# A block of ffn, two mixers and ffn on one core: first unit's weights beside the input, written places for the norm's sums, gates' sigmoids among pair 0's products

## The chip, the cores and the metric

One NeuronCore of a Trainium2 chip runs the kernel. The time is that of the device for one execution, in microseconds (us); smaller is better. Each figure of a kernel's time is the median of several executions. The engines carry the names of the profile: PE is TensorE (PEld its loads of the stationary operand), ACT ScalarE, DVE VectorE, POOL GpSimd, and SP SyncE, which here only issues DMAs.

## What is computed

One layer, `x` with 512 frames of 1024 numbers, all in fp32:

```python
x = x + 0.5 * swiglu(rms_norm(x, ffn1_norm), ffn1_w1, ffn1_w3, ffn1_w2)   # silu(h@w1)*(h@w3) @ w2, 2816 hidden
h = rms_norm(x, mix_norm)
p = h @ w_in                      # r, k, v (512 each), codes w, a, g; FoX q, k, v, f; gates (2048)
p_rwkv = token_shift(p[:, :SHIFT_COLS], shift_mu)        # u + (prev - u) * mu
y_a = rwkv7_mixer(p_rwkv, ...) @ rwkv_proj               # 8 heads of 64, delta-rule state
y_b = fox_mixer(p[:, SHIFT_COLS:...], ...) @ fox_proj    # attention with forget gates
x = x + (sigmoid(g_a) * y_a + sigmoid(g_b) * y_b) @ w_out
x = x + 0.5 * swiglu(rms_norm(x, ffn2_norm), ffn2_w1, ffn2_w3, ffn2_w2)
return rms_norm(x, final_norm)
```

In the RWKV mixer the decay is made from `w0 + tanh(w_code) @ w_up`, and `a = sigmoid(a0 + a_code @ a_up)`. The kernel makes the first through a sigmoid too: these two groups, four column blocks each, are its eight "pz" products.

## The kernel before

All activations lie transposed: a column block `c` of x is a tile of 128 features by 512 frames, and there are eight. A product is exact to fp32 by splitting: each operand is a high part in fp32r and the low part that is left, and `mm3` (L124 to L127) issues three matmuls, high by high (L125), high weight by low activation (L126), low weight by high activation (L127). A product of 128 columns of a weight matrix with the eight blocks is thus 24 matmuls of 512 columns (`Norm.cols`, L203). Its weights come by `load_raw` (L104: one DMA on SP's queue into one of 3 buffers "raw") and `split_w` (L113: ACT casts the high part "whi" at L117, DVE subtracts the low part "wlo" at L118; 2 buffers each).

The order of work on each engine is set by a scheduler that simulates the program and issues what is ready; `tc.issue_after(x)` holds an instruction behind x, `keep_in_program_order` holds a row of them in written order.

- **Start (L216 to L372).** Seven warm products on PE (L219). Then the first hidden unit of ffn1 (128 columns of w1 in the PSUM bank f0, of w3 in f1) is made column block by column block while x arrives. Every instruction of this block passes through `Queued` (L228, recorded at L234), which chains the instructions of one engine in the written order. `turn(c)` transposes block c of x on PE (tile xtp, four transposes); `x_copy` copies it to SBUF on ACT (xT); `x_hi` makes the high part xh (even blocks on DVE, odd ones on ACT) and `x_lo` the low part xl on DVE, both scaled by the norm's gain and read from xtp; `w_hi`, `w_lo` split the unit's weights by halves; `mul(i, c)` issues the three matmuls of block c on bank i. `square` and `add` sum the squares for the norm (acc). The first unit's raw and split weights take buffers of the same rings as all others.
- **ffn1 (L430 to L492).** Unit j has pa (w1) and pb (w3). Its scale by the norm (rstd) is applied behind the product, in `hidden`, so the sum of squares over the features is only needed then: `Norm.finish` (L193) splits acc (`exact`, L135: shi on ACT, slo on DVE), sums it by two matmuls with ones (ssum, L139 and L140), and makes rstd by Ln and Exp on ACT. `finish` is called behind pa of unit 1; where its two matmuls stand among the products is the scheduler's choice. `during` loads 18 small parameter rows (L399 to L415) on SP's queue at unit 2. After 22 units come eight products with w2 (pd), whose results go into x and, by `mix_add`, into the next norm's operands.
- **Mix (L537 to L581).** `mix.finish`, the products of the codes (pl, 72 and 96 columns), then the eight pz (L579), each read by a sigmoid on ACT (L580), kept in that order, and behind them the table load for Ln and Exp (L581). PSUM has 8 banks: 2 in the pool pm (pl, pk, pgt, pa, pd), 3 in pr (pb, ssum, one half of the pz), 3 in pf (the other half).
- **Pairs (`step`, L634).** For each of four pairs of heads: `column` (L611) makes the products k, r, v (tile pk), each scaled by rstd into u (L614, DVE) and shifted in time (L532 on ACT, L533 on DVE); a gate product pgt follows. The sigmoids' results are summed along time by DVE (scan, L650, with the mask cmask that POOL sets at L588, L589), exponentials follow on ACT (L655, L656), and keys and queries go to the tiles BK and G, which the products gp (L694) read.

Behind this come the recurrence with the attention, the projections, ffn2 (the same `ffn`, with `finish` behind unit 0) and the last norm.

## Time and profile before

| | |
|---|---|
| median of 3 executions | 1208.77 us (1207.17 to 1209.34) |
| the profiled execution | 1206.81 us, of which the span of the trace is 1205.1 us |
| mean granted clock of PE | 0.997 |
| moved by DMA | 122.54 MB, 102 GB/s |
| ffn1's first unit ends, its pa of unit 1 begins | 23.55 us |
| last pd of ffn1 ends, pl begins | 380.34 us |
| pair 0: first k product / first gate product | 392.27 / 414.42 us |
| recurrence begins | 561.33 us |

A row of a timeline has: start in us, length in us, engine, line of the code, operation, tiles (out<-in), shape, xcount, and in brackets how long the engine was idle just before and what released it. In a group's row the idle time before and its releasers stand behind the bar. A matmul's length in the timeline overlaps with the next one's; the distance of starts is its pace.

### The profile page before, as it was taken

The numbers are of one execution on the slowest core, as the hardware profiler recorded it, in microseconds if no ns is written. First come the engines' busy times: TensorE is split into PE (matmuls) and PEld (weight loads), VectorE is DVE, ScalarE is ACT, GpSimd is POOL, SyncE is SP. The second block draws the span as 40 slices with busy tenths as digits, with TensorE's granted clock in tenths as the row PEclk, the third lists the DMA queues.
The fourth block names the chain that finished last, engine by engine and source line by source line (L and its number), as shares of the span: only waits on it lengthen the run. The fifth ranks groups of instructions, "written<-read, shape, count | busy, mean of one in ns | idle before, by whom it ended". The sixth has DMA issues, their size and how long they took to land.

```text
span 1205.1 us, 15863 instructions
## 1 busy us (share of the span) xinstructions
PE 1183.4 (98%) x6332; PEld 950.3 (79%) x6332; DVE 661.5 (55%) x990; ACT 454.9 (38%) x733; POOL 94.7 (8%) x141
## 2 busy tenths in 40 slices
PE   8999999999999999999999999999999999999997
PEld 6788888888887788887767776778888888888887
DVE  6554445443334788686756655766554545543232
ACT  5322222222223754346876655523222222222221
POOL 2100000001111111311000011111000000000110
PEclk9999999999999999999999999999999999999999
DMA  6333333323333334345112135633323233323331
GB/s 183 90 101 95 97 105 88 103 81 114 114 114 93 94 101 116 114 127 129 40 56 89 54 97 164 192 106 88 105 88 105 88 105 91 102 84 92 96 97 71
DMA packets 210296, 122.54 MB, mean 102 GB/s; under 512 B 9998, under 2 KB 202574, under 8 KB 210222
## 3 DMA queue, kind: packets, MB, share of 16 engines
q1 hardware_dynamic: 204222, 108.67, 31.0%
q0 software_dynamic: 3760, 12.06, 3.1%
q8 instruction: 50, 0.82, 0.3%
q10 hardware_dynamic: 2240, 0.79, 0.3%
q14 instruction: 24, 0.20, 0.1%
HBM read 110.82 MB, written 10.68 MB: 101 GB/s over the span
## 4 chain that ended last, share of the span: by engine, by line
PE 93%; DVE 3%; ACT 1%; issue 1%; DMA 0%; DVEq 0%; ACTq 0%
PE pd L127 7%; PE pd L126 7%; PE pd L125 7%; PE pb L127 6%; PE pb L125 6%; PE pb L126 6%; PE pa L127 6%; PE pa L126 6%; PE pa L125 6%; PE pgt L125 3%; PE pgt L127 2%; PE pgt L126 2%; PE pk L125 2%; PE pk L127 2%; PE pk L126 2%; PE ppj L125 1%
## 5 line engine op out<-in xcount | busy, mean ns | idle before, releaser
L117 ACT CAST whi<-raw 128x1024 fp32r<-128x1024 f32 (+2 forms) x196 | 195.2, 997 | 617.7 <-PE pa L126 176.6
L118 DVE TENSOR_TENSOR wlo<-raw,whi 128x1024 fp32r<-128x1024 f32 (+2 forms) x196 | 227.0, 1158 | 136.9 <-ACT whi L117 136.9
L125 PE MATMUL pb<-xh,whi 128*128 128x512 f32 x344 | 134.0, 390 | 1.2 <-ACT whi L117 1.2
L127 PE MATMUL pa<-xh,wlo 128*128 128x512 f32 x344 | 134.2, 390 | 0.8 <-DVE wlo L234 0.5
L127 PE MATMUL pb<-xh,wlo 128*128 128x512 f32 x344 | 134.0, 389 | 0.5 <-DVE wlo L118 0.5
L125 PE MATMUL pa<-xh,whi 128*128 128x512 f32 x344 | 134.0, 389 | 0.2 <-ACT whi L234 0.2
L126 PE MATMUL pa<-xl,whi 128*128 128x512 f32 x344 | 133.9, 389 | 0.0
L126 PE MATMUL pb<-xl,whi 128*128 128x512 f32 x344 | 133.8, 389 | 0.0
L127 PE MATMUL pd<-hh,wlo 128*128 128x512 f32 x330 | 130.8, 396 | 0.0
L125 PE MATMUL pd<-hh,whi 128*128 128x512 f32 x330 | 130.3, 395 | 0.0
L126 PE MATMUL pd<-hl,whi 128*128 128x512 f32 x330 | 130.3, 395 | 0.0
L439 DVE TENSOR_TENSOR fb<-pb,rstd 128x512 f32<-128x512 f32 x43 | 29.7, 691 | 133.7 <-PE pb L127 133.7
L125 PEld LDWEIGHTS pb<-xh,whi 128*128 128x128 f32 x344 | 64.5, 188 | 15.3 <-ACT whi L117 2.0
L127 PEld LDWEIGHTS pa<-xh,wlo 128*128 128x128 f32 x344 | 64.5, 188 | 15.1 <-DVE wlo L234 1.0
L127 PEld LDWEIGHTS pb<-xh,wlo 128*128 128x128 f32 x344 | 64.6, 188 | 14.4 <-DVE wlo L118 1.0
L125 PEld LDWEIGHTS pa<-xh,whi 128*128 128x128 f32 x344 | 64.6, 188 | 14.0 <-ACT whi L234 0.7
L126 PEld LDWEIGHTS pa<-xl,whi 128*128 128x128 f32 x344 | 64.6, 188 | 13.4
L126 PEld LDWEIGHTS pb<-xl,whi 128*128 128x128 f32 x344 | 64.6, 188 | 13.4
L126 PEld LDWEIGHTS pd<-hl,whi 128*128 128x128 f32 x330 | 62.0, 188 | 14.9
L125 PEld LDWEIGHTS pd<-hh,whi 128*128 128x128 f32 x330 | 62.0, 188 | 14.6
L127 PEld LDWEIGHTS pd<-hh,wlo 128*128 128x128 f32 x330 | 62.0, 188 | 14.6
L435 DVE TENSOR_TENSOR fa<-pa,rstd 128x512 f32<-128x512 f32 x43 | 29.7, 692 | 73.2 <-PE pa L127 73.2
(380 smaller groups left out, 1960.7 us busy)
## 6 DMA issues: line engine op xcount, KB each, us to landing
raw<-in_ffn_w_dram SPq DMA_DIRECT2D x116, 512.0 KB
raw<-in_w_in_dram SPq DMA_DIRECT2D x40, 512.0 KB
raw<-in_ffn_w_dram SPq DMA_DIRECT2D x15, 384.0 KB
raw<-in_w_out_dram SPq DMA_DIRECT2D x8, 512.0 KB
raw<-in_ffn_w_dram SPq DMA_DIRECT2D x9, 256.0 KB
gsave<-gs SPq DMA_DIRECT2D x9, 256.0 KB
xin<-in_x_dram SPq DMA_DIRECT2D x8, 256.0 KB
xsave<-xT POOLq DMA_DIRECT2D x8, 256.0 KB, 2.3
```

Source lines behind the costliest of these rows:

```text
L117: (hi_eng or act).copy(hi[:], raw[:])
L118: (eng or dve).tensor_tensor(lo[:], raw[:], hi[:].bitcast(F32), op=ALU.subtract)
L125: pe.matmul(ps, whi, xhi, start=first, stop=False)
L126: pe.matmul(ps, whi, xlo, start=False, stop=False)
L127: return pe.matmul(ps, wlo, xhi, start=False, stop=last)
L435: dve.tensor_tensor(a[:], pa[:], nrm.rstd[:], op=ALU.mult)
L439: dve.tensor_tensor(b[:], pb[:], nrm.rstd[:], op=ALU.mult)
```

## The change

Three edits.

**First unit.** Its raw and split weights get tiles of their own in the pool x0, so the rings of `load_w` are free: w1 and w3 of unit 1 are loaded right behind the input, and both are split within the queued block. For blocks 2 to 7 ACT copies xtp to SBUF first, and xh and xl are made from the copy. The transposes run one block ahead (`turn(4)` before `mul(0, 2)`), and the squares come later. Five warm products in place of seven. The parameter rows are issued behind the last weight load that stands before them in the program.

**Norm sums.** `finish` is divided: `parts` adds, casts and subtracts; `finish(behind)` issues both ssum matmuls behind a given matmul, and the next product is issued behind them (`[summed]`, the holes of `cols`). The places: ffn1 behind the last but one matmul of pa of unit 1, mix behind pl's 72 columns, ffn2 behind pa of unit 0.

**Pair 0.** Its products k and r are written ahead of the pz, and pz i is issued behind the matmul i of r (`spread`); `step(0)` no longer makes them.

How PE's order stands in the first unit before: xtp are the transposes of a block, f0 and f1 the two banks, xh2 and xl2 the parts of block 2.

```order
L234 MATMUL xtp_212<-ident_78,xin3_136 128x128 x4
L234 MATMUL f0_147<-xh2_202,whi_143 128x512
L234 MATMUL f0_147<-xl2_204,whi_143 128x512
L234 MATMUL f0_147<-xh2_202,wlo_145 128x512
L234 MATMUL f1_148<-xh2_202,whi_144 128x512
L234 MATMUL f1_148<-xl2_204,whi_144 128x512
L234 MATMUL f1_148<-xh2_202,wlo_146 128x512
L234 MATMUL xtp_230<-ident_78,xin4_137 128x128 x4
L234 MATMUL f0_147<-xh3_223,whi_143 128x512
```

And in the changed kernel, from the same place:

```order
L244 MATMUL xtp_210<-ident_78,xin3_134 128x128 x4
L244 MATMUL xtp_215<-ident_78,xin4_135 128x128 x4
L244 MATMUL f0_145<-xh2_201,fwhi0_141 128x512
L244 MATMUL f0_145<-xl2_203,fwhi0_141 128x512
L244 MATMUL f0_145<-xh2_201,fwlo0_143 128x512
L244 MATMUL f1_146<-xh2_201,fwhi1_142 128x512
L244 MATMUL f1_146<-xl2_203,fwhi1_142 128x512
L244 MATMUL f1_146<-xh2_201,fwlo1_144 128x512
L244 MATMUL xtp_231<-ident_78,xin5_136 128x128 x4
L244 MATMUL f0_145<-xh3_227,fwhi0_141 128x512
```

Two blocks are transposed before the products of block 2, and from there on each transpose stands a block further ahead.

On SP's queue three weight loads (w3 of unit 1, w1 and w3 of unit 2) now stand between w1 of unit 1 and the first of the parameter rows; before, the rows followed w1 of unit 1 directly.

PE at the end of pair 0's r product before (pk_2943 is r, pk_2993 is v):

```order
L579 MATMUL pz_2851<-codes_2734,uw_330 128x512
L579 MATMUL pz_2857<-codes_2734,uw_330 128x512
L579 MATMUL pz_2863<-codes_2734,uw_330 128x512
L127 MATMUL pk_2943<-xh7_2709,wlo_2947 128x512
L579 MATMUL pz_2869<-codes_2734,uw_330 128x512
L579 MATMUL pz_2872<-codes_2734,ux_331 128x512
L125 MATMUL pk_2993<-xh0_2052,whi_2996 128x512
L126 MATMUL pk_2993<-xl0_2053,whi_2996 128x512
```

And in the changed kernel (pk_2884 is r, pk_2991 v, pgt_3026 the gate):

```order
L129 MATMUL pk_2884<-xh7_2707,wlo_2888 128x512
L604 MATMUL pz_2919<-codes_2732,uw_338 128x512
L604 MATMUL pz_2922<-codes_2732,ux_339 128x512
L604 MATMUL pz_2925<-codes_2732,uw_338 128x512
L604 MATMUL pz_2928<-codes_2732,ux_339 128x512
L604 MATMUL pz_2931<-codes_2732,uw_338 128x512
L604 MATMUL pz_2934<-codes_2732,ux_339 128x512
L127 MATMUL pk_2991<-xh0_2050,whi_2994 128x512
L128 MATMUL pk_2991<-xl0_2051,whi_2994 128x512
...
L604 MATMUL pz_2937<-codes_2732,uw_338 128x512
L129 MATMUL pk_2991<-xh7_2707,wlo_2995 128x512
L127 MATMUL pgt_3026<-xh0_2050,whi_3029 128x512
L604 MATMUL pz_2940<-codes_2732,ux_339 128x512
L128 MATMUL pgt_3026<-xl0_2051,whi_3029 128x512
```

Six pz follow r's last matmul; the seventh stands ahead of v's last matmul and the eighth behind the gate's first.

ACT at the same place before (whi_2996 is v's weights, whi_3031 the gate's; L580 the sigmoids, L532 the shift's first half):

```order
L117 CAST whi_2996<-raw_2994 128x1024
L117 CAST whi_3031<-raw_3029 128x1024
L580 ACTIVATE G30_2728<-pz_2851,par_116 128x512
L580 ACTIVATE G30_2728<-pz_2854,par_116 128x512
L580 ACTIVATE G31_2729<-pz_2857,par_116 128x512
L580 ACTIVATE G31_2729<-pz_2860,par_116 128x512
L580 ACTIVATE BK3_2733<-pz_2863,par_116 128x512
L580 ACTIVATE BK3_2733<-pz_2866,par_116 128x512
L580 ACTIVATE spare0_2736<-pz_2869,par_116 128x512
L580 ACTIVATE spare0_2736<-pz_2872,par_116 128x512
L581 ACT_TABLE_LOAD
L532 ACTIVATE spare1_2737<-u_2923,omu_2744 128x512
```

And in the changed kernel (whi_3029 is the gate's, whi_3120 those of pair 1's k; L605 the sigmoids):

```order
L119 CAST whi_3029<-raw_3027 128x1024
L550 ACTIVATE spare1_2735<-u_2915,omu_2742 128x512
L605 ACTIVATE G30_2726<-pz_2919,par_116 128x512
L605 ACTIVATE G30_2726<-pz_2922,par_116 128x512
L605 ACTIVATE G31_2727<-pz_2925,par_116 128x512
L605 ACTIVATE G31_2727<-pz_2928,par_116 128x512
L605 ACTIVATE BK3_2731<-pz_2931,par_116 128x512
L605 ACTIVATE BK3_2731<-pz_2934,par_116 128x512
L119 CAST whi_3120<-raw_3118 128x1024
L605 ACTIVATE spare0_2734<-pz_2937,par_116 128x512
L605 ACTIVATE spare0_2734<-pz_2940,par_116 128x512
L606 ACT_TABLE_LOAD
```

The gate's cast and the shift of r stand ahead of the sigmoids, and a cast stands between the sixth and the seventh.

The diff, cut to its core:

```diff
+    loads = []
+
     def load_raw(aps, kt, n):
         raw = wp.tile([P, kt, n], F32, tag="raw", name="raw", bufs=3)
         for c0, src in aps:
-            nc.sync.dma_start(raw[:, :, c0:c0 + src.shape[1]],
-                              src.rearrange("(k p) c -> p k c", p=P))
+            loads.append(nc.sync.dma_start(raw[:, :, c0:c0 + src.shape[1]],
+                                           src.rearrange("(k p) c -> p k c", p=P)))
         return raw
...
-        def finish(s):
+        def parts(s, a=act, v=dve):
+            if s.last is not None:
+                v.tensor_tensor(s.acc[:], s.acc[:], s.last[:], op=ALU.add)
+            s.sum = tmp("shi", dt=F32R), tmp("slo", dt=F32R)
+            a.copy(s.sum[0][:], s.acc[:])
+            v.tensor_tensor(s.sum[1][:], s.acc[:], f32(s.sum[0][:]), op=ALU.subtract)
+
+        def finish(s, behind):
             ps = bank("ssum", pr)
-            if s.last is not None:
-                dve.tensor_tensor(s.acc[:], s.acc[:], s.last[:], op=ALU.add)
-            exact(ps[:], onesr, s.acc[:])
+            with tc.issue_after(behind.ins):
+                for i in range(2):
+                    done = pe.matmul(ps[:], onesr[:], s.sum[i][:], start=i == 0, stop=i == 1)
             ln = tmp("rln")
             ln_act(ln[:], ps[:], bias=epsr[:, 0:1], scale=1.0 / D)
             s.rstd = xp.tile([P, T], F32, tag="rstd", name="rstd")
             act.activation(s.rstd[:], ln[:], AF.Exp, scale=-0.5)
+            return done
...
     warm = bank("warm", pf)
-    for _ in range(7):
+    for _ in range(5):
         pe.matmul(warm[:, 0:P], ones[:], ones[:], start=True, stop=True)
...
         xin = [x0.tile([P, NB, P], F32, name=f"xin{c}") for c in range(KD)]
-        fraw = [wp.tile([P, KD, P], F32, tag="raw", name="raw", bufs=3) for _ in range(2)]
-        fhi, flo = [[wp.tile([P, KD, P], F32R, tag=f"w{n}", name=f"w{n}", bufs=2) for _ in range(2)] for n in ("hi", "lo")]
+        fraw = [x0.tile([P, KD, P], F32, name=f"fraw{i}") for i in range(2)]
+        fhi, flo = [[x0.tile([P, KD, P], F32R, name=f"fw{n}{i}") for i in range(2)] for n in ("hi", "lo")]
         first = [bank(f"f{i}") for i in range(2)]
...
             nrm.hi[c] = xp.tile([P, T], F32R, tag=f"xh{c}", name=f"xh{c}")
+            from_ = (xps if c < 2 else xT)[c][:]
             if c % 2:
-                qact.activation(nrm.hi[c][:], xps[c][:], AF.Copy, scale=pc(PAR_FFN1 + c))
+                qact.activation(nrm.hi[c][:], from_, AF.Copy, scale=pc(PAR_FFN1 + c))
             else:
-                qdve.tensor_scalar(nrm.hi[c][:], xps[c][:], pc(PAR_FFN1 + c), None, op0=ALU.mult)
+                qdve.tensor_scalar(nrm.hi[c][:], from_, pc(PAR_FFN1 + c), None, op0=ALU.mult)
         def x_lo(c):
             nrm.lo[c] = xp.tile([P, T], F32R, tag=f"xl{c}", name=f"xl{c}")
-            qdve.scalar_tensor_tensor(nrm.lo[c][:], xps[c][:], pc(PAR_FFN1 + c), f32(nrm.hi[c][:]),
+            from_ = (xps if c < 2 else xT)[c][:]
+            qdve.scalar_tensor_tensor(nrm.lo[c][:], from_, pc(PAR_FFN1 + c), f32(nrm.hi[c][:]),
                                       op0=ALU.mult, op1=ALU.subtract)
...
         x_copy(1)
+        x_copy(2)
         x_hi(2)
         x_lo(2)
-        x_copy(2)
         square(0)
         square(1)
         add()
         turn(3)
+        turn(4)
         mul(0, 2)
         mul(1, 2)
+        x_copy(3)
         x_hi(3)
         x_lo(3)
-        x_copy(3)
+        turn(5)
+        mul(0, 3)
+        mul(1, 3)
+        x_copy(4)
+        x_hi(4)
+        x_lo(4)
         w_hi(0, 1)
         w_hi(1, 1)
-        turn(4)
-        mul(0, 3)
-        mul(1, 3)
-        x_hi(4)
-        x_lo(4)
-        x_copy(4)
         w_lo(0, 1)
         w_lo(1, 1)
-        square(2)
-        turn(5)
...
-        x_copy(7)
+        add()
+        second = [split_w(load_raw([(0, ffn1_w1[0][:, P:2 * P])], KD, P), KD, P, qdve, hi_eng=qact)]
         mul(0, 7)
         mul(1, 7)
-        for c in range(4, KD):
+        for c in range(3, KD):
             square(c)
             add()
         nrm.last = None
+        nrm.parts(qact, qdve)
+        second.append(split_w(load_raw([(0, ffn1_w3[0][:, P:2 * P])], KD, P), KD, P, qdve, hi_eng=qact))
...
                 for ps, w in ((pa, w1), (pb, w3)):
-                    wh, wl = first[1] if j == 1 and first and ps is pa else load_w([(0, w[0][:, c0:c0 + P])], KD, P)
-                    nrm.cols(ps[:], wh, wl, P)
-                    if ps is pa and j == 1 and first:
-                        nrm.finish()
-                        hidden(0, *first[0])
-                if j == 0:
-                    nrm.finish()
+                    if j == 1 and first:
+                        wh, wl = first[1][ps is pb]
+                    else:
+                        wh, wl = load_w([(0, w[0][:, c0:c0 + P])], KD, P)
+                    mms = nrm.cols(ps[:], wh, wl, P, [summed] if summed else [])
+                    summed = None
+                    if ps is pa and nrm.rstd is None:
+                        if first is None:
+                            nrm.parts()
+                        summed = nrm.finish(mms[-1 if first is None else -2])
+                        if first:
+                            hidden(0, *first[0])
                 if j in during:
-                    with tc.issue_after(pin.ins):
+                    with tc.issue_after(pin.ins), tc.issue_after(loads[-1].ins):
                         during[j]()
...
-    ffn(nrm, ffn1_w1, ffn1_w3, ffn1_w2, mix_add, {2: load_params, 4: masks, 10: place_params}, (first, ahead))
+    ffn(nrm, ffn1_w1, ffn1_w3, ffn1_w2, mix_add, {2: load_params, 4: masks, 10: place_params}, (first, second))
...
-        mix.finish()
+        psa, psg = bank("pl"), bank("pl")
+        mms = mix.cols(psa[0:72, :], *load_w([(0, W[:, COL_W:COL_W + 64]), (64, W[:, COL_F:COL_F + 8])], KD, 72), 72)
+        mix.parts()
+        summed = mix.finish(mms[-1])
         tc.keep_in_program_order(act.preload_act_table_set("sigmoid_and_others"))
-        psa, psg = bank("pl"), bank("pl")
-        mix.cols(psa[0:72, :], *load_w([(0, W[:, COL_W:COL_W + 64]), (64, W[:, COL_F:COL_F + 8])], KD, 72), 72)
-        mix.cols(psg[0:96, :], *load_w(win(COL_G, 96), KD, 96), 96)
+        mix.cols(psg[0:96, :], *load_w(win(COL_G, 96), KD, 96), 96, [summed])
         rc = rp.tile([P, NB], F32, name="rc")
...
         zslots = [h.rearrange("p c a t -> p (c a t)") for h in zslots] + spare[0:2]
+        spread = []
+        for o, c0, mu in ((spare[2], DA, 4), (spare[3], 0, 0)):
+            ps = bank("pk")
+            spread = mix.cols(ps[:], *load_w(win(c0), KD, P), P)
+            shifted(o, normed(ps), P, PAR_MU + mu)
         za = []
         for p in range(NP):
             za.append((zslots[2 * p], zslots[2 * p + 1]))
             for i, (w_, x_, par0, o) in enumerate(((uw, lw, PAR_W0, zslots[2 * p]), (ux, lx, PAR_A0, zslots[2 * p + 1]))):
                 ps = bank("pz", (pr, pf)[i])
-                pe.matmul(ps[:], w_[0:96, p * P:(p + 1) * P], x_[0:96, :], start=True, stop=True)
+                with tc.issue_after(spread[2 * p + i].ins):
+                    pe.matmul(ps[:], w_[0:96, p * P:(p + 1) * P], x_[0:96, :], start=True, stop=True)
                 tc.keep_in_program_order(act.activation(o, ps[:], AF.Sigmoid, bias=pc(par0 + p)))
...
             BK = BKs[p]
-            column(DA, p, k, 4)
+            if p:
+                column(DA, p, k, 4)
             kk = prep("kk", p)
...
-            mms = column(0, p, r, 0)
+            mms = column(0, p, r, 0) if p else spread
             ps = bank("pn", pf)
```

More of the change, by code (lines that the diff above doesn't have):

```diff
@@ L325 @@
         turn(3)
+        turn(4)
         mul(0, 2)
         mul(1, 2)
+        x_copy(3)
         x_hi(3)
         x_lo(3)
-        x_copy(3)
+        turn(5)
[4 more added lines that the diff above has]
+        x_lo(4)
         w_hi(0, 1)
         w_hi(1, 1)
-        turn(4)
-        mul(0, 3)
-        mul(1, 3)
-        x_hi(4)
-        x_lo(4)
-        x_copy(4)
         w_lo(0, 1)
         w_lo(1, 1)
-        square(2)
-        turn(5)
+        turn(6)
         mul(0, 4)
         mul(1, 4)
+        x_copy(5)
         x_hi(5)
         x_lo(5)
-        x_copy(5)
-        add()
-        square(3)
-        turn(6)
+        turn(7)
         mul(0, 5)
         mul(1, 5)
+        x_copy(6)
         x_hi(6)
         x_lo(6)
-        x_copy(6)
-        add()
-        turn(7)
+        square(2)
         mul(0, 6)
         mul(1, 6)
+        x_copy(7)
         x_hi(7)
         x_lo(7)
-        ahead = split_w(load_raw([(0, ffn1_w1[0][:, P:2 * P])], KD, P), KD, P, qdve, hi_eng=qact)
-        x_copy(7)
+        add()
+        second = [split_w(load_raw([(0, ffn1_w1[0][:, P:2 * P])], KD, P), KD, P, qdve, hi_eng=qact)]
         mul(0, 7)
         mul(1, 7)
-        for c in range(4, KD):
+        for c in range(3, KD):
             square(c)
```

1 line of the change is left out of this document (added).

## The prediction

> **What bounds the kernel now.** I read the first part of the page (busy time by engine) and the chain that ended last, then the busy time by stretch, and then the timeline of the stretches in which TensorE isn't full.
>
> ```profile
> span 1205.1 us, 15863 instructions
> PE 1183.4 (98%) x6332; PEld 950.3 (79%) x6332; DVE 661.5 (55%) x990; ACT 454.9 (38%) x733; POOL 94.7 (8%) x141
> PE 93%; DVE 3%; ACT 1%; issue 1%; DMA 0%; DVEq 0%; ACTq 0%
> ```
>
> PE carries 93% of the chain: only PE time taken out of the span counts. The view by stretch, in us: length, then busy time (instructions) of PE, PEld, DVE, ACT, POOL, then the granted clock.
>
> ```profile
> 10.43:23.55 13.12, 12.19 (x58) 8.59 (x56) 8.23 (x14) 8.83 (x16) 0.00 (x0) 1.00 0.67 171
> 23.55:51.03 27.48, 24.85 (x103) 18.68 (x103) 17.13 (x22) 13.94 (x18) 8.48 (x7) 1.00 0.30 85
> 404.45:414.42 9.97, 8.31 (x29) 6.00 (x28) 7.78 (x9) 9.92 (x17) 2.57 (x10) 0.83 0.23 64
> 414.42:500.00 85.58, 85.58 (x535) 69.81 (x534) 73.91 (x102) 46.94 (x63) 19.72 (x30) 1.00 0.35 104
> ```
>
> Busy PE time includes waits inside the pipeline, so I count starts. A gate product (24 matmuls of 512 columns) starts at the first of these rows, the next product at the second:
>
> ```profile
> 414.42 0.39 PE L125 MATMUL pgt<-xh,whi 128*128 128x512 f32 x1
> ...
> 419.86 0.39 PE L125 MATMUL pk<-xh,whi 128*128 128x512 f32 x1
> ```
>
> 5.44/24 = 0.227 us for each, the pitch of a full PE. Four transposes and one matmul lie between the first and third of these rows:
>
> ```profile
> 10.65 0.60 PE L234 MATMUL xtp<-ident,xin 128*128 128x128 f32 x4
> 11.01 0.48 PE L234 MATMUL f<-xh,whi 128*128 128x512 f32 x1
> 11.32 0.40 PE L234 MATMUL f<-xl,whi 128*128 128x512 f32 x1
> ```
>
> 0.67 − 0.227 = 0.44 for four, 0.11 each. The counts of the stretches hold instructions that still run from before the border: one, one and two. So the work and the loss are:
>
> - 10.43 to 23.55: 37 × 0.227 + 20 × 0.11 = 10.6 of 13.12: **2.5 lost**
> - 23.55 to 51.03: 102 × 0.227 = 23.15 of 27.48: **4.3 lost**
> - 404.45 to 414.42: 27 × 0.227 = 6.13 of 9.97: **3.8 lost**
>
> These 10.6 us are all that the change can aim at; in the stretch from 414.42 PE is busy throughout.
>
> **First unit.** What waits there:
>
> ```profile
> 13.73 0.50 PE L234 MATMUL f<-xl,whi 128*128 128x512 f32 x1 [0.32 <-DVE xl L234]
> 21.87 0.50 PE L234 MATMUL f<-xl,whi 128*128 128x512 f32 x1 [0.28 <-DVE xl L234]
> 23.55 0.50 PE L125 MATMUL pa<-xh,whi 128*128 128x512 f32 x1 [0.24 <-ACT whi L234]
> 24.81 0.50 PE L127 MATMUL pa<-xh,wlo 128*128 128x512 f32 x1 [0.53 <-DVE wlo L234]
> 37.36 0.50 PE L125 MATMUL pb<-xh,whi 128*128 128x512 f32 x1 [0.94 <-ACT whi L117]
> 38.62 0.50 PE L127 MATMUL pb<-xh,wlo 128*128 128x512 f32 x1 [0.53 <-DVE wlo L118]
> 13.71 0.59 ACT L234 COPY xT<-xtp 128x512 f32<-128x512 f32 x1 [0.84 <-DVE xl L234]
> ```
>
> The first two wait for the low part of a column of x, the next four for split weights. The last row shows a cost of the old order: the copy stood idle behind DVE's reading of the same PSUM tile. The prices (all in the last number but one: count, total and mean ns, or min/median/max):
>
> ```profile
> L234 ACT COPY xT<-xtp 128x512 f32<-128x512 f32 x8 | 4.6, 588 | 4.1 <-DVE xl L234 4.1
> L234 ACT ACTIVATE xh<-xtp,par 128x512 fp32r<-128x512 f32 x4 | 2.7, 686 | 1.7 <-PE xtp L234 1.7
> L171 DVE TENSOR_SCALAR xh<-xT,par 128x512 fp32r<-128x512 f32 x8 | 3.9, 485 | 0.2
> L172 DVE SCALAR_TENSOR_TENSOR xl<-xT,par,xh x8: 742/1781/1781, 275.0 to 383.2; 128x512 fp32r<-128x512 f32 x8
> L234 DVE TENSOR_TENSOR wlo<-raw,whi 128x512 fp32r<-128x512 f32 x3 | 2.0, 683 | 0.0
> ```
>
> Now a column goes copy, high, low: 0.59 + 0.69 + 0.74 = 2.0 us, one copy longer than from PSUM. But a transpose runs one column ahead: between it and its first product stand two columns' products and one or two transposes, 12 × 0.227 + 0.44 = 3.2 us, where before there was one column's 6 × 0.227 + 0.44 = 1.8. That covers 2.0 with 1.2 left. Throughput holds too: for two columns in 3.6 us, ACT has two copies, one high part and two half casts of 0.62 (the 128x1024 one of 1.05 for a half more), 3.1; DVE two low parts, one high part and two 0.68 subtractions, 3.35. That is tight in DVE, once; I leave 0.4 of the 2.5.
>
> The low part's price hangs on POOL: 742 ns alone, 1781 in most runs of ffn1's end. In 10.43 to 23.55 POOL has no instruction, so I take 0.74; at 1.78 DVE would need 5.4 in 3.6 us, and six columns would cost up to 6 × 0.9 = 5.4 us. The Trainium skill, "SBUF — State Buffer", section "Who interferes with whom", says that a VectorE instruction with two SBUF inputs contends with a GpSimd instruction that reads SBUF. This speaks against reading the copy instead of PSUM; the trace agrees in kind (742 against 1781), and where POOL is empty the rule gives the same 0.74.
>
> The weights of units 1 and 2 then load directly behind the input, ahead of the small parameter rows, which take SP's queue from here to the second line's end:
>
> ```profile
> 10.90 1.72 SPq L399 DMA_DIRECT2D rows<-in_mix_norm_dram  x1
> ...
> 22.25 0.42 SPq L415 DMA_DIRECT2D loraw<-in_rwkv_a_up_dram  x1
> ```
>
> PE: first unit ends at 10.43 + 10.6 + 0.4 = 21.4; pa of unit 1 (5.4) 26.9, where the two ssum matmuls stand; pb must have its low weights at 27.8. ACT after the last column: one cast, five squares, the sum's cast, the second cast: 1.05 + 5 × 0.63 + 0.62 + 1.05 from about 20, so 26; DVE's 1.23 ends at 27.5. I put 0.2 for this. So 6.8 − 0.4 − 0.2 = **6.2 us gained**. The fourth of these loads waits for one of the three raw buffers, free when DVE has split unit 1's w1, about 21.5; behind it on SP stand the parameter rows, which took 22.67 − 10.90 = 11.8, so until 33.3, and then unit 3's w1. That is needed at 26.9 + 0.45 + 3 × 5.44 = 43.7; with 3.1 to land (an estimate: its 128x1024 numbers, 0.52 MB, at the 171 GB/s of 10.43 to 23.55) and 1.05 + 1.23 of splitting, 5.0 are left.
>
> **Warm products, 7 to 5.** PE waits for x there (first row), so nothing is gained. The clock shows 1.00 early, and 0.50 in one stretch of 3.41 us:
>
> ```profile
> 8.31 0.42 PEld L234 LDWEIGHTS xtp<-ident,xin 128*128 128x128 f32 x4 [0.34 <-DMA xin<-in_x_dram]
> ...
> 4.22:7.65 3.43, 2.39 (x14) 1.55 (x12) 2.27 (x4) 1.23 (x3) 0.34 (x2) 1.00 1.05 295
> 407.00:410.41 3.41, 2.91 (x7) 2.33 (x8) 2.30 (x4) 3.39 (x6) 2.03 (x9) 0.50 0.58 159
> ```
>
> If five products let the first stretch fall to half, its 2.39 us of busy PE would cost up to 2.4, part of it under the wait for x; I take 0. The Trainium skill, "TensorE: Matmul & The Clock Gate", Part 1, "What's actually happening", has the clock at half until a free-running window of 3413 ns was busy, which speaks against fewer warm products; the last row agrees in length, and no run here shows five.
>
> **Mix.** Before, the seventh and eighth pz found no free bank until a sigmoid had run, and v's product none until r's u was made:
>
> ```profile
> 403.95 1.05 ACT L117 CAST whi<-raw 128x1024 fp32r<-128x1024 f32 x1 [3.39 <-PE pk L126]
> 404.91 2.42 ACT L580 ACTIVATE G<-pz,par 128x512 f32<-128x512 f32 x4
> 405.64 0.50 PE L579 MATMUL pz<-codes,uw 96*128 96x512 f32 x1 [0.79 <-ACT G L580]
> 406.75 1.29 DVE L614 TENSOR_TENSOR u<-pk,rstd 128x512 f32<-128x512 f32 x2 [0.49 <-PE pz L579]
> 407.50 0.79 PE L125 MATMUL pk<-xh,whi 128*128 128x512 f32 x1 [0.78 <-DVE u L614]
> 409.65 1.28 ACT L581 ACT_TABLE_LOAD   x1
> ```
>
> Now k and r of pair 0 precede all pz; six find the six free banks, and the seventh and eighth stand a whole product later, behind v, when four sigmoids have long freed theirs. v's bank needs only k's u, 6 us old. So the waits at 405.64 and 407.50 go, and with them the half clock (5 × 0.2 of the 3.8). In their place: on ACT, the cast for the gate waits for r's last reader and stands ahead of the sigmoids; the next cast waits for v's last reader and stands ahead of the last two. Sigmoids: 404.9 + 6 × 0.605 = 408.5, the cast after v 409.9 to 411, two more to 412.2, table load to 413.5, 2.6 later than before's 410.93. Queued behind are pair 0's exponentials and POOL's mask, which waits for the last pz. I leave 0.3: **3.5 gained**. The ssum of the mix, and of ffn2, stand at places where PE didn't stall on them: 0 (±0.3). Behind pair 0, PE's order is the same up to ffn2 but for some rows, so what PE gains by then stays gained unless a buffer comes late.
>
> Sum: 6.2 + 3.5 = 9.7. The profiled execution took 1206.81 (span 1205.1), 1.96 under the median of the three runs; a difference carries over: 1208.77 − 9.7 = **1199.1**.
>
> **Rivals.**
> - *The mix's gain is given back in pair 0* (chance 0.17). Pair 0's keys and their first reader:
>
> ```profile
> 430.43 0.70 DVE L673 TENSOR_TENSOR BK<-kka,Tall 128x512 f32<-128x512 f32 x1
> ...
> 435.65 1.15 PE L694 MATMUL gp<-G,BK 64*64 64x64 f32 x32
> ```
>
>  The keys are there at 431.13, 4.5 us ahead of their reader. PE comes 3.5 earlier, less five rows (1.1) that the order puts ahead of gp, and ACT's chain 2.6 later: 4.5 − 2.4 − 2.6 is −0.5 if nothing is absorbed. At most all 3.5 go: 1202.6. For it: DVE is 86% busy there. Against: r's and k's own steps now lie earlier.
> - *SP's rows hold up unit 3's weights* (0.05): if they last over 11.8 + 5.0 = 16.8 us; at 21 unit 3 comes 4 us late: 1203.1. For it: the queue stands in their way now, and other transfers run beside them. Against: the rows are a few KB.
> - *The change does not do what it says* (0.04): ACT or DVE sets its pace whatever PE's order, and the splits of unit 1 come as late: 6.2 lost, with the rival above 9.7: no change, 1208.8.
> - *Slower* (0.03): DVE becomes the bound from 414.42 to 500. It has 73.91 of 85.58; four scans (4.7) move into it: 78.6. It decides once over 7 us more are added. If each of POOL's 19.72 us there blocked DVE, 98.3: 12.7 over, 1208.77 − 9.7 + 12.7 = 1211.8. Against: the durations already hold what POOL cost in this stretch.
>
> **Numbers.** A measurement of this kernel can tell about 0.2% (2.4 us) from no change. Forecast 1199.1, chance 0.71; own range 1196.5 to 1201.5: the 0.9 that I left and one run's spread (1207.17 to 1209.34) below; the warm-up's 2.4 above. The first two rivals reach 1203.1. Range: 1196.0 to 1203.2, leaving out 0.07 and the tails of the forecast. Faster by over 0.2%: 0.71 + 0.17 + 0.05 = 0.93; same 0.04; slower 0.03.
>
> **What would show it.** Right: pa of unit 1 starts near 21.5, unit 3's near 44, with no wait of over 0.3 us for split weights; the clock at 1.00 through the mix; k, r and v of pair 0 back to back, the pgt's first matmul about 10 us earlier than 414.42. Wrong: xl of 1.78 in the first unit; a half clock before 8 us; gp with a wait for BK or G in pair 0; a pa of unit 3 that waits for its cast; a sum of the two gains under 7.

## The result, and the profile after

The changed kernel takes 1199.54 us (median of 5 executions, 1198.3 to 1199.84); the kernel before took 1207.61 beside it (5 executions, 1206.85 to 1209.34). The ratio on record is 0.9923, 95% interval 0.9912 to 0.9934: 9.3 us faster, 8.0 to 10.6. It is not the ratio of these two medians, which lie 8.1 apart. The forecast was 1199.1, 9.7 faster.

The first part of the page of the changed kernel, and the chain that ended last:

```profile
span 1196.7 us, 15846 instructions
PE 1179.2 (99%) x6328; PEld 951.4 (79%) x6328; DVE 660.8 (55%) x990; ACT 454.4 (38%) x733; POOL 93.2 (8%) x141
PE 94%; DVE 3%; DMA 1%; ACT 1%; issue 0%; SPq 0%; DVEq 0%; ACTq 0%
```

The span is 8.4 us shorter, and PE's share of the chain went from 93% to 94%; the shares of DVE and ACT read the same as before, 3% and 1%. Three places of PE's timeline say where the time went (the first pa behind the first unit, the first pl, the last of them the first xps of the recurrence):

```profile
22.88 0.40 PE L127 MATMUL pa<-xh,whi 128*128 128x512 f32 x1
...
375.50 0.39 PE L127 MATMUL pl<-xh,whi 128*72 128x512 f32 x1
...
552.68 0.33 PE L888 MATMUL xps<-RD,G 128*32 128x64 f32 x8
```

Before they stood at 23.55, 380.34 and 561.33. So 4.84 us are gained up to pl (forecast 6.2), 3.81 from pl to the recurrence (forecast 3.5), and 0.26 are given back behind it: 8.39. (That way takes 637.12 before and 637.38 now; the spread of it is shown below.)

**First unit and ffn1.** None of the waits that the prediction listed is left. The view by stretch of the changed kernel (length, busy PE, PEld, DVE, ACT, POOL, granted clock) shows most of what kept 4.84 from being 6.2:

```profile
5.05:8.46 3.41, 1.78 (x9) 1.25 (x10) 2.37 (x4) 1.74 (x4) 0.00 (x0) 1.00 1.14 311
8.46:11.87 3.41, 3.41 (x12) 2.83 (x12) 2.70 (x5) 2.64 (x6) 0.00 (x0) 0.50 1.22 291
```

PE runs at half clock in the second of two stretches of 3.41 us, behind one in which it was busy for about half the time. (The expectations below put this at 8.2 to 11.6.) Its timeline ahead of it and in it, and the end of pa of unit 1 with the two sum matmuls:

```profile
6.36 0.50 PE L244 MATMUL f<-xh,fwhi 128*128 128x512 f32 x1 [1.48 <-ACT fwhi L244]
...
10.08 0.63 PE L244 MATMUL f<-xh,fwhi 128*128 128x512 f32 x1
10.51 0.63 PE L244 MATMUL f<-xl,fwhi 128*128 128x512 f32 x1
10.94 0.63 PE L244 MATMUL f<-xh,fwlo 128*128 128x512 f32 x1
11.36 0.63 PE L244 MATMUL f<-xh,fwhi 128*128 128x512 f32 x1
...
28.35 0.39 PE L206 MATMUL ssum<-shi,onesr 128*128 128x512 f32 x1
28.59 0.39 PE L206 MATMUL ssum<-slo,onesr 128*128 128x512 f32 x1
28.81 0.40 PE L127 MATMUL pb<-xh,whi 128*128 128x512 f32 x1
29.05 0.40 PE L128 MATMUL pb<-xl,whi 128*128 128x512 f32 x1
29.45 0.50 PE L129 MATMUL pb<-xh,wlo 128*128 128x512 f32 x1
```

The matmuls from 10.08 on start 0.43 apart in place of 0.227. The first row is the first product of block 0, which waited for its split weight. Further down the sums cost no stall, and pb's low weights come 0.17 late (29.45 − 29.05 − 0.227): the thin place for which the prediction left 0.2.

**Mix.** The pz and v's product in the changed kernel:

```profile
399.35 0.39 PE L604 MATMUL pz<-codes,uw 96*128 96x512 f32 x1
399.58 0.39 PE L604 MATMUL pz<-codes,ux 96*128 96x512 f32 x1
399.81 0.40 PE L127 MATMUL pk<-xh,whi 128*128 128x512 f32 x1
400.04 0.40 PE L128 MATMUL pk<-xl,whi 128*128 128x512 f32 x1
...
405.05 0.40 PE L604 MATMUL pz<-codes,uw 96*128 96x512 f32 x1
405.51 0.39 PE L127 MATMUL pgt<-xh,whi 128*128 128x512 f32 x1
405.74 0.40 PE L604 MATMUL pz<-codes,ux 96*128 96x512 f32 x1
```

No start is more than 0.24 behind the one before it, and there is no half clock. The rest of ACT's and DVE's chain, and the reader gp:

```profile
405.24 1.05 ACT L119 CAST whi<-raw 128x1024 fp32r<-128x1024 f32 x1 [1.72 <-PE pk L128]
406.20 1.26 ACT L605 ACTIVATE spare<-pz,par 128x512 f32<-128x512 f32 x2
407.48 1.28 ACT L606 ACT_TABLE_LOAD   x1
...
424.96 0.68 DVE L699 TENSOR_TENSOR BK<-kka,Tall 128x512 f32<-128x512 f32 x1
...
428.23 1.15 PE L720 MATMUL gp<-G,BK 64*64 64x64 f32 x32
```

The cast that waits for v stands ahead of the last two sigmoids, as the order said; the table load ends at 408.76, 2.67 after before's 410.93 once the 4.84 of ffn1 are added back (forecast 2.6). BK is written at 425.64, 2.6 before gp: the rival of pair 0 did not decide.

### The profile page after: what moved, and what is told of

Its sections match the earlier page's. It is cut to its first block, busy times and chain, and to the rows that moved or that the text cites. A ratio compares the mean times of both kernels' runs of the same rounds, so it can differ in the third digit from the quotient of the medians.

```text
span 1196.7 us, 15846 instructions
## 1 busy us (share of the span) xinstructions
PE 1179.2 (99%) x6328; PEld 951.4 (79%) x6328; DVE 660.8 (55%) x990; ACT 454.4 (38%) x733; POOL 93.2 (8%) x141
## 4 chain that ended last, share of the span: by engine, by line
PE 94%; DVE 3%; DMA 1%; ACT 1%; issue 0%; SPq 0%; DVEq 0%; ACTq 0%
PE pd L129 7%; PE pd L128 7%; PE pd L127 7%; PE pb L129 7%; PE pa L129 7%; PE pb L128 7%; PE pa L128 7%; PE pa L127 7%; PE pb L127 7%; PE pgt L127 3%; PE pgt L129 2%; PE pgt L128 2%; PE pk L127 2%; PE pk L128 2%; PE pk L129 2%; PE pw L129 1%
## 5 line engine op out<-in xcount | busy, mean ns | idle before, releaser
L119 ACT CAST whi<-raw 128x1024 fp32r<-128x1024 f32 (+3 forms) x195 | 194.1, 996 | 620.5 <-PE pa L128 177.8
L120 DVE TENSOR_TENSOR wlo<-raw,whi 128x1024 fp32r<-128x1024 f32 (+3 forms) x195 | 225.9, 1159 | 120.2 <-ACT whi L119 120.2
```

Of the source, the lines that this page charges most:

```text
L119: (hi_eng or act).copy(hi[:], raw[:])
L120: (eng or dve).tensor_tensor(lo[:], raw[:], hi[:].bitcast(F32), op=ALU.subtract)
```

## The experiments

The 12 runs were timed in three groups, each beside the kernel before on its chip (medians 1207.66, 1209.57 and 1207.83). Three places of each profile, in us: the first pa (the first unit's end), the way from pl to the first xps, and the way from xps to PE's last matmul.

| kernel | time (range) | ratio (95%) | first pa | pl to xps | xps to end | half clock at |
|---|---|---|---|---|---|---|
| before | 1207.61 (1206.85–1209.34) | 1 | 23.55 | 180.99 | 637.12 | 407 |
| changed | 1199.54 (1198.3–1199.84) | 0.9923 (0.9912–0.9934) | 22.88 | 177.18 | 637.38 | 8.5 |
| again | 1198.14 (1197.2–1200.16) | 0.9918 (0.9903–0.9934) | 21.06 | 177.23 | 638.86 | 613 |
| warm7 | 1198.73 (1196.46–1200.09) | 0.9918 (0.9905–0.9931) | 21.58 | 177.20 | 638.98 | 613 |
| fill | 1198.44 (1197.63–1198.95) | 0.9917 (0.9905–0.993) | 22.12 | 177.24 | 638.10 | 615 |
| nopair | 1199.0 (1198.22–1200.73) | 0.9925 (0.9912–0.9938) | 21.91 | 178.33 | 637.74 | start |
| paironly | 1205.36 (1203.38–1207.61) | 0.9975 (0.9966–0.9984) | 25.28 | 177.26 | 638.92 | start, 622 |
| nosums | 1199.28 (1198.05–1199.57) | 0.992 (0.9906–0.9933) | 22.18 | 177.27 | 639.10 | start, 614 |
| mixold | 1200.21 (1199.75–1200.66) | 0.9929 (0.9917–0.9942) | 22.27 | 179.16 | 637.78 | start |
| noahead | 1201.28 (1200.41–1201.55) | 0.9937 (0.9924–0.9949) | 24.09 | 177.22 | 637.46 | start |
| nocopy | 1198.61 (1197.99–1200.46) | 0.9918 (0.9905–0.9932) | 23.12 | 177.21 | 639.22 | start, 615 |
| rowsfirst | 1198.98 (1197.78–1199.43) | 0.9921 (0.9907–0.9934) | 20.93 | 177.21 | 638.75 | 613 |
| delay4 | 1199.11 (1199.1–1199.56) | 0.9924 (0.9911–0.9938) | 23.32 | 177.30 | 637.49 | start |
| delay8 | 1197.54 (1194.04–1198.35) | 0.9906 (0.9892–0.992) | 23.78 | 177.12 | 636.33 | start, 613 |

"Start" means that PE is at half pace from its first products on until 9 to 13 us: the transposes of block 2 of x, at 8 to 10 us, start 0.21 apart (0.14 in nopair, where the half pace ends among them), where 0.109 is the full pace.

### Is it the warm products? (warm7, fill, again)

warm7 undoes one line of the change; fill puts eight dummy products into the two early gaps of PE; again is the changed kernel itself.

```diff
-    for _ in range(5):
+    for _ in range(7):
```

> The changed kernel with seven warm products again instead of five. Its profile shows PE at half clock from about 8.2 to 11.6 us, behind a stretch in which PE was idle for 1.5 us; before shows none. Theory: the two missing products thinned the window that decides, so with seven the half clock goes and the first unit ends about 1.5 us earlier in the profile; time 1198.0 against 1199.5. Rival: the windows lie differently in each run, and two products less at 1.4 to 4.4 us do not touch the window that decides (4.8 to 8.2); then same time as the changed kernel within 0.4, and the half clock comes or not as the windows fall.

```diff
         turn(0)
+        for _ in range(6):
+            qpe.matmul(warm[:, 0:P], ones[:], ones[:], start=True, stop=True)
         x_hi(0)
...
         mul(0, 0, (1, 2))
+        for _ in range(2):
+            qpe.matmul(warm[:, 0:P], ones[:], ones[:], start=True, stop=True)
         x_lo(1)
```

> The changed kernel with six more warm products behind the transposes of block 0 and two more behind its products, where PE otherwise waits for the first split weights and for xh of block 1. Theory (the idle time between 4.7 and 6.4 us brings the half clock from 8.2 on): the clock stays at 1.00 and the pa of unit 1 starts at about 21.4 instead of 22.9; time about 1198.0. Rival (it hangs on where the windows fall, not on this gap): half clock in some place of the first 12 us all the same, time 1199.5 or a little more, since the fillers can stand in the way by up to 0.3.

> The changed kernel, word for word, on the chip of the next three. It is there for the clock: in its first profile PE ran at half clock from 8.2 to 11.6 us, and the four variants so far had that stretch elsewhere (in the recurrence) or nowhere. If the half clock falls where the windows happen to lie, this profile shows it at another place or not at all, pa of unit 1 then starts at about 21.7 instead of 22.9, and the times spread over 1196.5 to 1200; if it belongs to the five warm products, it is at 8 to 12 us again and no time is under 1198.

In again the same program has its half clock elsewhere. Two stretches of it, at 8 us and in the recurrence, and then its first pa:

```profile
8.00:11.40 3.40, 3.40 (x22) 2.89 (x22) 2.75 (x5) 2.97 (x7) 0.00 (x0) 1.00 1.22 291
612.83:616.00 3.17, 3.17 (x14) 2.10 (x12) 2.60 (x7) 1.26 (x5) 0.00 (x0) 0.50 0.00 0
```

```profile
21.06 0.40 PE L127 MATMUL pa<-xh,whi 128*128 128x512 f32 x1
```

So the half clock is no fixed part of the changed kernel: one execution has it at 8.5, another at 613, and pa of unit 1 starts at 22.88 or at 21.06. Of these 1.82, 1.47 are the half clock (from the fourth product of the unit to block 3's transposes it is 8.08 to 12.30 in the changed kernel's first profile, 7.72 to 10.47 in again). The other 0.36 stood there before it: the first split weight came late, and the first product started at 6.36 in place of 5.82. Eight profiles have the changed kernel's first unit unaltered (changed, again, rowsfirst, nosums, mixold, nopair, delay4, delay8): two reach pa at 20.93 and 21.06 with block 2 transposed at full pace, six at 21.91 to 23.78 with a half clock in some of the first 13 us. In five of these six it lasts from PE's first products on; only the changed kernel's first profile goes to full pace and falls back. With seven products (before, warm7, paironly) two of three are free of it. That leans to the theory of the warm products without settling it, and the time cannot tell: warm7's ratio of 0.9918 lies in again's interval.

The two products have a price of their own, though, which shows where the clock is alike. Block 0's transposes and its first product, in again and then in warm7:

```profile
3.77 1.11 PE L244 MATMUL xtp<-ident,xin 128*128 128x128 f32 x4
5.82 0.47 PE L244 MATMUL f<-xh,fwhi 128*128 128x512 f32 x1 [0.94 <-DVE xh L244]
```

```profile
4.62 1.03 PE L244 MATMUL xtp<-ident,xin 128*128 128x128 f32 x4
6.59 0.47 PE L244 MATMUL f<-xh,fwhi 128*128 128x512 f32 x1 [0.94 <-DVE xh L244]
```

With seven the transposes start 0.85 later, behind the warm products and not behind x, and of this 0.5 is left at pa (21.58 against 21.06 and rowsfirst's 20.93). These are single profiles.

fill was at full pace from 7.10 on, but its products held back the first product of block 0, which waited behind them until 7.10 in place of 5.82:

```profile
6.60 0.76 PE L244 MATMUL warm<-ones 128*128 128x128 f32 x3
7.10 0.49 PE L244 MATMUL f<-xh,fwhi 128*128 128x512 f32 x1
```

What it saved there it paid there; pa at 22.12 shows neither the 21.4 of the theory nor the half clock of the rival.

### What is the mix's gain made of? (nopair, paironly, nosums, mixold)

nopair undoes the third edit; paironly puts it alone into the kernel before.

```diff
-        spread = []
-        for o, c0, mu in ((spare[2], DA, 4), (spare[3], 0, 0)):
...
-                with tc.issue_after(spread[2 * p + i].ins):
-                    pe.matmul(ps[:], w_[0:96, p * P:(p + 1) * P], x_[0:96, :], start=True, stop=True)
+                pe.matmul(ps[:], w_[0:96, p * P:(p + 1) * P], x_[0:96, :], start=True, stop=True)
...
-            if p:
-                column(DA, p, k, 4)
+            column(DA, p, k, 4)
...
-            mms = column(0, p, r, 0) if p else spread
+            mms = column(0, p, r, 0)
```

> The changed kernel without its third edit: pair 0's k and r are made in the pair's own step and the pz stand as before. Theory (the edits add up, each in its stretch): the waits at the pz and at v return with the half clock behind them, 3.5 to 3.8 us; time 1203.2, and the distance from pl's first matmul to pair 0's gp as before, 55.3 instead of 52.7. Rival (pair 0's work eats part of it later, or the two gains overlap): less than 2.5 slower than the changed kernel.

> The kernel before with the third edit alone (pair 0's k and r ahead of the pz). Theory: 3.5 to 3.8 us faster than before, 1203.9; first unit and ffn1 as before (pa of unit 1 at 23.6, pl at 380.3), no half clock in the mix. Rival (the third edit needs the written place of the mix's norm sum to pay): 1206 or more.

The theory of nopair fell: the way from pl to xps grew by 1.15, not by 3.5. Only one of before's waits came back, that of v's product for r's u:

```profile
399.16 0.40 PE L598 MATMUL pz<-codes,ux 96*128 96x512 f32 x1
400.34 0.50 PE L127 MATMUL pk<-xh,whi 128*128 128x512 f32 x1 [0.78 <-DVE u L633]
```

1.18 from start to start, 0.95 over the pitch. paironly on the other hand has the whole 3.73 there (177.26) without the second edit. Its time is 3.0 us better than before by the ratio (1.9 to 4.1), with a median between the 1203.9 of its theory and the 1206 of its rival; its profile says nothing on the first unit, whose end at 25.28 was late by a half clock at the start. So each edit alone seems to remove most of it, which the next two kernels test. nosums lets the scheduler place the sums again:

```diff
-            with tc.issue_after(behind.ins):
-                for i in range(2):
-                    done = pe.matmul(ps[:], onesr[:], s.sum[i][:], start=i == 0, stop=i == 1)
+            for i in range(2):
+                done = pe.matmul(ps[:], onesr[:], s.sum[i][:], start=i == 0, stop=i == 1)
...
-        summed = mix.finish(mms[-1])
```

> The changed kernel with the norm's two sum matmuls placed by the scheduler again (in the mix they stand among the second code product, 14 matmuls later; in ffn2 the second one 19 later; in ffn1 nothing moves). Theory (in the mix edits two and three stand for each other, each removes the same waits): pl to the recurrence's first xps stays at 177.2 within 0.4, time as the changed kernel. Rival (the written place pays by itself): 1 us or more longer there.

mixold is nosums and nopair together.

> The changed kernel with edits two and three undone in the mix: pair 0's products in the pair's step and the sums placed by the scheduler, so that PE's order there is nearly that of before, behind the changed start. Theory of the overlap: the waits at the pz and at v return, 2.4 us in all, with up to 1.4 more where the half clock falls behind them; pl to xps 179.6 to 181.0 (before 180.99, without edit three alone 178.33, changed 177.18), time 1201.5 to 1203. Rival (without edit three alone the mix lost only 1.15 because that run had no half clock, and the sums do nothing): pl to xps 178.3 as without edit three alone, time as that one, 1199.

From pl to xps: both edits undone 179.16, sums placed 178.33 (0.83 gained), pair 0 moved 177.27 (1.89 gained), both 177.18 (1.98). They overlap: with pair 0 moved, the sums' place is worth 0.09. mixold's wait is the same one, a little longer:

```profile
399.62 0.51 PE L597 MATMUL pz<-codes,ux 96*128 96x512 f32 x1
400.91 0.50 PE L127 MATMUL pk<-xh,whi 128*128 128x512 f32 x1 [0.78 <-DVE u L632]
```

It missed the expected 179.6 by 0.4 and the expected 1201.5 by 1.3, since the wait at the pz did not come back and no half clock fell there. Of before's 180.99, then, 1.83 lie beyond what these edits' order explains in a run without half clock. Six starts from 407.50 on, 0.2 to 0.36 over the pitch, make up 1.36 in all, of which the half clock has about 1.3 (0.11 of the first is what the start behind that wait costs in mixold too); the 0.5 left are the net of the wait at the pz and of small waits in other places, in an order of PE that differs by some rows.

### What is the first unit's gain made of? (noahead, nocopy, rowsfirst)

noahead puts each transpose behind the products that it had been moved ahead of:

```diff
         turn(3)
-        turn(4)
         mul(0, 2)
...
-        turn(5)
+        turn(4)
         mul(0, 3)
```

> The changed kernel with each block of x transposed directly ahead of the products of the block before it, as in the kernel before, the copy still first. Working of the prediction: between a transpose and its first product there is 1.8 us again, and copy, high and low part take 2.0, so each of five blocks waits 0.2 to 0.5 us: pa of unit 1 1.0 to 2.5 us later than without the edit, 22.7 to 24.2 where no half clock falls; time 1 to 2 us longer. Rival (DVE or the arrival of x sets the pace, not the distance): within 0.4 us of 21.7.

```profile
14.67 0.50 PE L244 MATMUL f<-xl,fwhi 128*128 128x512 f32 x1 [0.15 <-DVE xl L244]
...
22.83 0.50 PE L244 MATMUL f<-xl,fwhi 128*128 128x512 f32 x1 [0.29 <-DVE xl L244]
...
31.21 0.50 PE L129 MATMUL pb<-xh,wlo 128*128 128x512 f32 x1 [0.43 <-DVE wlo L244]
```

The waits for the low part are back, over the pitch 0.41 and 0.11 at block 3, 0.27 at block 5 and 0.2 and 0.56 at block 7, and the split of unit 1's w3 is late as well (0.6 over the pitch in place of again's 0.18). Pa starts at 24.09, inside the 22.7 to 24.2 expected, though a half clock at the start has a part in that: up to block 3's transposes noahead is already 1.38 behind again (11.85 against 10.47), and the waits behind them are the other 1.6. 1201.28 against 1198.14 on the same chip is the largest loss of the steps that were undone one by one, and holds that half clock too.

nocopy reads the parts of blocks 2 to 7 from PSUM again.

```diff
-            from_ = (xps if c < 2 else xT)[c][:]
+            from_ = xps[c][:]
```

> The changed kernel with the high and low parts of blocks 2 to 7 read from the transposes' PSUM tile, as before, the copy still first and the transposes a block ahead; no instruction moves. By the prediction the source has no price of its own: from PSUM the high part takes 0.75 on DVE against 0.48 from the copy, the low part the same, and neither need wait for the copy; with 3.2 us between a transpose and its products both fit. pa of unit 1 at 21.1 to 22.9 as the changed kernel's own profiles, no stall over 0.3 us from 12 to 22; same time within 0.5. Rival (two engines that read one PSUM tile go one after the other, as the copy's idle 0.84 behind xl in the profile before suggests): 1 us or more longer.

```profile
13.67 0.70 ACT L244 ACTIVATE xh<-xtp,par 128x512 fp32r<-128x512 f32 x1
...
14.40 0.75 DVE L244 SCALAR_TENSOR_TENSOR xl<-xtp,par,xh 128x512 fp32r<-128x512 f32 x1 [0.87 <-ACT xh L244]
15.07 0.74 DVE L244 TENSOR_SCALAR xh<-xtp,par 128x512 fp32r<-128x512 f32 x1
```

From 11 us to pa PE has no wait, and the ratio is again's: with the transposes a block ahead, where the parts are read from costs nothing. Pa at 23.12 comes from the half clock at the start and from block 1 of x, for which PE waited 0.53 at 7.19.

rowsfirst sets 18 small loads between w1 and w3 of unit 1.

```diff
+        dummy = x0.tile([4, 18, P], F32, name="dummy")
+        for i in range(18):
+            nc.sync.dma_start(dummy[:, i], rwkv_w0[0].rearrange("(a b) -> a b", b=P))
         second.append(split_w(load_raw([(0, ffn1_w3[0][:, P:2 * P])], KD, P), KD, P, qdve, hi_eng=qact))
```

> The changed kernel with 18 more small row loads on SP's queue between w1 and w3 of unit 1, into a tile that nothing reads: the place that the parameter rows held before (two of those were larger). Theory (the late weights of unit 1 are what ffn1's start lost, 2.5 of its 4.3 us): w3 leaves SP at about 17 and lands after 20 in place of 17.7, which its cast behind the sum's at 27 doesn't notice; but unit 2's w1 and w3 and then the rows go some 6 us later too, so unit 3's w1 is issued at 36 instead of 30.6; it has until 42, and lands at 39: no more than 0.5 us of wait. Rival (the queue has no slack): 3 us or more at pa of unit 3.

```profile
10.61 9.01 SPq L383 DMA_DIRECT2D dummy<-in_rwkv_w_dram  x18
19.66 2.18 SPq L109 DMA_DIRECT2D raw<-in_ffn_w_dram  x3
...
31.24 15.52 SPq L109 DMA_DIRECT2D raw<-in_ffn_w_dram  x5
```

Two weight loads leave SP 8 to 9 us later than in again; the next waits for its buffer in both. From 11 to 45 us PE has no wait but the 0.19 at pb's low weights, which again has too. Unit 3's w1 is issued 2.3 later than again's 28.94. So the forecast of at most 0.5 held, but the theory behind it, by which the late weights of unit 1 lost 2.5 us of ffn1's start, gets no support: in the changed kernel the place of the rows on SP's queue is worth nothing. From the first pa to pl PE takes 356.79 before and 357.69 in paironly, but 352.62 to 352.68 in changed, again, nosums and rowsfirst, so the 4.1 gained there belong to the first edit; what gains there is either that the first unit's weights left the shared buffers or that both splits of unit 1 stand ahead in the queued block. The two were not tried apart.

### How tight is pair 0's chain? (delay4, delay8)

Four or eight copies stand on ACT ahead of the last two sigmoids:

```diff
             za.append((zslots[2 * p], zslots[2 * p + 1]))
+            for _ in range(4 if p == 3 else 0):
+                tc.keep_in_program_order(act.copy(zslots[6], mix.rstd[:]))
```

> The changed kernel with four copies of 512 columns more on ACT between the sixth and the seventh sigmoid of the pz, 2.2 us in all; the output is the same. It puts a price on the rival of the prediction that pair 0's chain gives the mix's gain back: in the changed kernel's profile BK is written 2.6 us before gp reads it. Theory: BK's writing moves by at most 2.2, gp waits for nothing, pl to xps 177.2 to 177.6, same time. Rival (the chain is tight in some other place, the scans or the casts behind them): 1 us or more longer there.

> As the last, with eight copies, 4.4 us and more; the scheduler moves some 100 rows of PE's order for it. Theory: past the 2.6 us of slack the waits come, 1.8 to 3 us longer from pl to xps (179 to 180). Rival (the queue of other products that the scheduler finds hides it): under 178.

The table load, BK's writing and gp, of delay8:

```profile
415.06 1.28 ACT L608 ACT_TABLE_LOAD   x1
...
426.03 0.68 DVE L701 TENSOR_TENSOR BK<-kka,Tall 128x512 f32<-128x512 f32 x1
...
429.56 1.15 PE L722 MATMUL gp<-G,BK 64*64 64x64 f32 x32
```

From pl to xps delay4 takes 177.30 and delay8 177.12. delay4 agrees with the theory; delay8 refutes it. Its table load starts 38.6 behind pl (415.06 − 376.44), 6.6 later than the changed kernel's 32.0, and yet PE waits for nothing: BK is written 50.3 behind pl, where the changed kernel has 50.1, with only two rows more of PE ahead of gp. ACT took the copies up: work that needs no sigmoid stands among them, and the 2.61 us that ACT idles ahead of its cast at 416.89 in the changed kernel are gone. So the last two sigmoids do not set when BK is written, and the 2.6 between BK and gp is no price of theirs; the rival of pair 0 had less behind it than its 0.17. delay8's median of 1197.54 holds one execution of 1194.04; its interval meets the changed kernel's, so it is not shown to be faster.

## Why the prediction was right, point by point

- **What bounds the kernel:** PE, and only its gaps. Right: all that was gained lies in the three stretches named, and the time fell by what PE lost less of, 8.4 in the profiles, 8.1 between the medians and 9.3 by the ratio, against 9.7.
- **First unit, 6.2 us:** 4.84 in the changed kernel's first profile, 6.64 and 6.73 in again and rowsfirst, which are at full pace from the first product on (380.34 − 373.70 and − 373.61). Of again's 6.64, 2.49 lie in the first unit (forecast 2.1) and 4.15 behind it (forecast 4.1). The steps held: transposes a block ahead cover the 2.0 us of copy, high and low part (noahead); the low part at 0.75 with POOL idle (its rows in the changed kernel's first unit are all 0.75); the split of w3 0.17 late. One reason was idle: the order on SP's queue counts for nothing in the changed kernel (rowsfirst).
- **Warm products, "I take 0":** the step that failed, in both its halves. I read the granted clock as 1.00 from the start and so saw no price. About 1.5 us of half clock stood in the changed kernel's first profile, within the bound of 2.4 that I kept, and the sign of being wrong that I named, a half clock before 8 us, is there: block 0's transposes start 0.21 apart at 3.77, where before had them 0.11 apart. I also read PE as waiting for x there and so saw no gain; but block 0 waited for the warm products, and warm7 against again puts 0.5 us on two of them. Whether five products in place of seven make the half clock likelier stays open.
- **Mix, 3.5 us:** 3.81, as a sum right. As a working it was not: about 1.3 of the 3.8 counted as lost were a half clock that mixold, with the old order, did not have; and the norm sum's place, taken as 0, gains 0.83 by itself and 0.09 beside pair 0's move. Since both edits were made, the sum did not show it.
- **ffn2's sum, 0:** from ffn2's first pa to the end PE takes 368.99 in before, in the changed kernel and in nosums.
- **Rivals:** the mix's gain given back (0.17): no wait even with eight copies of 0.61 more on ACT. SP's rows (0.05): no wait. DVE as the bound (0.03): no sign; PE is busy throughout from 411 to 553.

## What to carry to other kernels

A kernel of this kind gains where PE waits for the preparation of its operands, and one cure shown here is distance: with the operand's source produced one block earlier, the low part's waits went (noahead has them back), and it no longer mattered which memory the parts were made from (nocopy). Before two edits in one stretch are added up, ask whether they remove the same wait; here each alone gave 0.83 and 1.89, both together 1.98. And of a stretch's lost time, take out what a half clock made before crediting the order of the work, since the next execution has it in another place.

## What the runs showed of the hardware

- The half clock moves between executions of one program: from 8.5 to 11.9 us in one, near 613 to 616 in the next. In the recurrence it costs about 1.4 us (xps to the end 638.1 to 639.2 with it, 637.1 to 637.8 without; delay8 with 636.33 stands outside of this). Eight of the eleven profiles with pair 0 moved have it there, none of the three without; whether the edit makes it likelier is open. The half clock may be behind part of the spread of 2 to 3 us within a kernel, but single executions have no profile to show it: warm7's two executions with a mean granted clock of 0.998 and 0.999 took 1196.46 and 1197.17, two with 0.997 1198.73 and 1199.8, a fifth with 0.998 1200.09.
- The column of the granted clock can miss a half clock at the start. In delay8 the view by stretch gives 1.00 from 10.4 to 12.5, and the timeline there has its matmuls 0.43 apart:

```profile
10.40:12.50 2.10, 2.10 (x6) 1.64 (x6) 1.22 (x3) 1.63 (x3) 0.00 (x0) 1.00 1.15 291
```

```profile
10.81 0.63 PE L244 MATMUL f<-xh,fwlo 128*128 128x512 f32 x1
11.24 0.63 PE L244 MATMUL f<-xh,fwhi 128*128 128x512 f32 x1
11.66 0.63 PE L244 MATMUL f<-xl,fwhi 128*128 128x512 f32 x1
```

The distance of starts is the surer sign.
- The Trainium skill, "TensorE: Matmul & The Clock Gate", Part 1, "What's actually happening", has the window free-running and the point of the change different from run to run. These runs agree: the stretch of half clock was 3.41 us long in before and in the changed kernel, and its place moved while the program did not.
